# More right-half pairs by seven products, quarter sums in place with a third raw tile, and second attention heads spread over more ticks

## The chip, the cores and the metric

The kernel runs on one core of one Trainium2 chip. The metric is device time in microseconds (us) of one execution. A core has five engines with queues of their own: TensorE (PE; its weight loads are listed as PEld), VectorE (DVE), ScalarE (ACT), GpSimd (POOL) and SyncE (SP), the last of which here only issues loads and stores. They meet through semaphores. Sixteen DMA engines move data between HBM and the on-chip memory.

## The reference

Two decoder layers on `x` of 256 tokens by 2048 columns, in float32:

```python
for l in range(DEPTH):                       # 2
    h = rmsnorm(x, attn_norm_g[l])
    q, k, v, gate_b, gate_c, conv_in = split(h @ w_in[l])       # 6 x 1024 columns
    q, k = rmsnorm over 64-wide half heads
    attn = diff_attention(q, k, v, lam, rel_bias)               # 8 heads, softmax1 - lam * softmax2, causal
    attn = rmsnorm(attn, subln_g[l]) * (1 - lam_init)
    conv = gate_b * short_conv3(gate_c * conv_in, conv_w[l])
    x = x + concat([attn, conv]) @ w_out[l]
    hm = rmsnorm(x, mlp_norm_g[l]) @ w_up[l]                     # 8192 columns
    x = x + square(relu(hm)) @ w_down[l]
```

## The kernel before

**Precision.** TensorE multiplies in a reduced form of float32, so every operand is split into a high part and the rest (ScalarE writes the high part, VectorE subtracts). A product is three terms (`TERMS`): high x high, high x low, low x high. Weights come from HBM as raw tiles and are split on the way: `whi`/`wlo` (L302, L303), `uhi`/`ulo` for w_up (L816, L817), `b1h`, `b2h`, `t13h`, `t24h` and their `l` parts for w_down by seven (L839, L840).

**A layer.** `mixer` runs q, k, v for the first four heads, then for the second four (`linear`, L386), then gate_C and conv_in in turn (`linear_t`: gc, ci, L408), gate_B (gb) and the output projection (o). `mlp` then runs the up stage and the right half.

**Background work.** TensorE's order is the order of the program, written by hand. Work that lies beside the main matmuls is a set of generators in `Background`; each `work.tick()` in a linear loop (16 in each `linear` and `linear_t`, 4 in each call of `columns`) counts the generators' waits down, and one that is due emits its next piece, its matmuls too, at that place. `attention` (with `pace` 1 for the first half of the heads, 2 for the second) runs four heads through `staggered`: each does its scores (`sc`), waits 10 ticks, transposes the probabilities (`ptp`), waits 4 ticks, multiplies by v (`av`); the last one also normalises all four (`an`) and after another wait transposes them into `cat` (`atp`). `Norm.chunk` makes a quarter of the next norm's tiles (`nT`). The order of the other engines is fixed when the program is built, by a simulated timeline; where `late` (`keep` in `quarters`) is used, it stays as written. Weight jobs are made `AHEAD` = 3 before they are taken.

**w_down by seven products.** The hidden columns are worked as 32 pairs of 128 (256 rows of w_down). For one pair, tokens in two halves and hidden rows in two halves make a 2 x 2 matrix of activations, and hidden rows by two stretches of 512 output columns a 2 x 2 matrix of weights. Their product takes eight products of 128 x 128 x 512, or seven after sums of quarters (a scheme like Strassen's). Each product is three matmuls, so an ordinary pair is 24 matmuls and one by seven is 21. `square` makes the sums of the activations once (L974 to L977). `quarters` makes those of the weights: `plain` loads the raw tile (L826, 1 MB) and splits b11 and b21, b22; `sums` computes t1, t3 (L853), t2 (L856) and t4 (L857) into a tile `t` with one buffer; `more` splits t2 and t4.

The left half of the output (`col` 0) is done during the up stage: 30 pairs by seven, two pairs behind the up columns (`LAG`), and the last two in the ordinary way. The hidden values are written to HBM (`hid`, or `hid7` for pairs that will go by seven on the right). In the right half they are read back: first pairs 30 and 31, then pairs 0 to 2 x `BLK` - 1 one by one (L1074 ordinary, L992 by seven, which pairs `SEVEN` lists), then the rest as blocks of two pairs by `columns` (L1143; `by_token`, L1131, for the last). `seven_onto` adds the seven accumulators to x (L1055, L1047, L1063). Read-back tiles `fb` come from `apool` (four buffers, shared with the norm tiles `nT`), the first block's from `fpool`. Raw tiles of w_down by seven come from `dpool` (`draw`, two buffers), those of w_up and of ordinary pairs from `upool` (`uraw`, four).

The pools of `mixer` and `mlp` use the same memory in turn, so the first loads of one wait for the last readers of the other.

Of the kernel before, what the change touches and what calls it, by code (L numbers as in the profile page):

```python
# [9 lines left out]
F32 = mybir.dt.float32  # L10
F32R = mybir.dt.float32r
# [4 lines left out]
P = 128  # L16
# [12 lines left out]
CH = 512  # L29
# [6 lines left out]
NB2 = DFF // (KG * P)  # L36


SEVEN = (2, 4, 7, 9, 12, 14, 17, 19, 22)
BLK = 12  # L40

TERMS = ((0, 0), (0, 1), (1, 0))
REL = 2 * S - P - 1
# [45 lines left out]
def staggered(pieces, apart):  # L89

    entries = [[i * apart, p] for i, p in enumerate(pieces)]
    while entries:
        for e in list(entries):
            if e[0] <= 0:
                try:
                    e[0] = max(1, next(e[1]))
                except StopIteration:
                    entries.remove(e)
                    continue
            e[0] -= 1  # L100
        if entries:
            yield 1
# [3 lines left out]
def trunk(ctx: ExitStack, tc: tile.TileContext, x, w_in, w_out, conv_w, q_norm_g, k_norm_g,  # L106
          lambda_q1, lambda_k1, lambda_q2, lambda_k2, subln_g, attn_norm_g, mlp_norm_g,
          w_up, w_down, rel_bias, selector, out):
    nc = tc.nc
# [3 lines left out]
    apool = ctx.enter_context(tc.tile_pool(name="apool", bufs=4))  # L113
# [12 lines left out]
    def bank(name):  # L126
        return ps.tile([P, CH], F32, tag="bank", name=name)

    def wide(name):
        return nat.tile([P, CH], F32, tag="wide", name=name)  # L130

    work = Background()
# [451 lines left out]
    def attention(l, qT, kT, kL, v, h0, dst, bias, tmp, pace):  # L584
# [3 lines left out]
        parts = dst.open()  # L588
# [5 lines left out]
        def unit(i):  # L594
            h = h0 + i
# [30 lines left out]
            for t in range(NT):  # L626
# [2 lines left out]
                                               nlam[:, l:l + 1], op0=ALU.mult, op1=ALU.mult)  # L629
                nc.vector.scalar_tensor_tensor(p[:, w], s[:, 1, w], c[:, t:t + 1], s[:, 0, w],  # L630
                                               op0=ALU.mult, op1=ALU.add)
            yield 10
            tp = bank(f"ptp{h}")
            for b in range(3):
                nc.tensor.transpose(tp[:, b * P:(b + 1) * P], p[:, b * P:(b + 1) * P], ident)
            pT = tmp.tile([P, 2, 3 * P], F32R, tag="pT", name=f"pT{h}", bufs=1)
            nc.scalar.activation(pT[:, 0], tp[:, :3 * P], AF.Copy)
            nc.vector.tensor_sub(pT[:, 1], tp[:, :3 * P], pT[:, 0].bitcast(F32))
            yield 4

            av = ps.tile([P, CH], F32, tag="av", name=f"av{h}", bufs=1)
            av = av.rearrange("p (t n c) -> p t n c", t=NT, n=2)
# [19 lines left out]
            f = rstd_of(flat, P, f"a{h0}", 4 * NT)  # L662
# [3 lines left out]
            for t in range(NT):  # L666
# [3 lines left out]
                    ao[:, t].rearrange("p (g d) -> p g d", d=P),  # L670
                    f2[:, :, t:t + 1].to_broadcast([P, 4, P]), op=ALU.mult)
                an_.append(an)
            yield 12 if pace == 1 else 18
            for t in range(NT):
                tp = bank(f"atp{h0}_{t}")
                for b in range(4):
# [7 lines left out]
                    op0=ALU.mult, op1=ALU.subtract)  # L684
                yield 2

        yield from staggered([unit(i) for i in range(4)], 8)
        dst.ready = True

    def conv(l, q, u, cv, norm):  # L690
# [99 lines left out]
    def mlp(l, mnorm, last):  # L790

        norm = None if last else Norm(0, l + 1)
        mT = mnorm.tiles
        with ExitStack() as scope:
            upool = scope.enter_context(tc.tile_pool(name="upool", bufs=4))
            fpool = scope.enter_context(tc.tile_pool(name="fpool", bufs=2))
            dpool = scope.enter_context(tc.tile_pool(name="dpool", bufs=2))
            spool = scope.enter_context(tc.tile_pool(name="spool", bufs=1))
            work.start(mnorm.factors(), 1)

# [2 lines left out]
            raws, forms = {}, {}  # L803
# [27 lines left out]
            def quarters(i, col=0):  # L831


                keep = late if i == 0 or (i == SEVEN[0] and col) else lambda ins: None

                def parts(src, tag, bufs):
                    hi = spool.tile(list(src.shape), F32R, tag=f"{tag}h", name=f"{tag}h", bufs=bufs)
                    lo = spool.tile(list(src.shape), F32R, tag=f"{tag}l", name=f"{tag}l", bufs=bufs)
                    keep(nc.scalar.activation(hi, src, AF.Copy))  # L839
                    keep(nc.vector.tensor_sub(lo, src, hi.bitcast(F32)))  # L840
                    return hi, lo

                def plain():
                    raw = forms["raw"] = load_rows(i, col).rearrange("p k (n c) -> p k n c", n=2)
                    h1, l1 = parts(raw[:, 0, 0], "b1", 2)
                    h2, l2 = parts(raw[:, 1], "b2", 2)
                    return (h1, l1), (h2[:, 0], l2[:, 0]), (h2[:, 1], l2[:, 1])

                def sums():
                    raw = forms["raw"]  # L850
                    t = forms["t"] = spool.tile([P, 4, CH], F32, tag="t", name="t")

                    keep(nc.vector.tensor_sub(t[:, 0:2], raw[:, :, 1], raw[:, 0]))  # L853
                    h, lw = parts(t[:, 0:2], "t13", 1)

                    keep(nc.vector.tensor_add(t[:, 2], t[:, 1], raw[:, 0, 0]))  # L856
                    keep(nc.vector.tensor_sub(t[:, 3], raw[:, 1, 0], t[:, 2]))  # L857
                    return (h[:, 0], lw[:, 0]), (h[:, 1], lw[:, 1])

                def more():  # L860
                    h, lw = parts(forms["t"][:, 2:4], "t24", 1)
                    return (h[:, 0], lw[:, 0]), (h[:, 1], lw[:, 1])

                if (i, col) == (0, 0):
                    made = {}
                    forms["plain"] = lambda: made.update(p=plain())
                    forms["sums"] = lambda: made.update(s=sums())
                    return lambda: made["p"], lambda: made["s"], more
                return plain, sums, more
# [21 lines left out]
            for i in range(NP - LAG, NP):  # L891
# [5 lines left out]

            order = [(b - n, n) for b in range(BLK, NB2) for n in range(2)
                     if BLK <= b - n < NB2 - 1]

# [12 lines left out]
            def blocks_of(order):  # L913
                for b, n in order:
                    box = []
                    four(b, n, 0, box)
                    four(b, n, 2, box)

            blocks_of([(NB2 - 1, 0), (NB2 - 1, 1)])
            for i in range(2 * BLK):  # L920
                if i in SEVEN:
                    weights.jobs += quarters(i, 2 * CH)
                    continue
                box = []
                for k in range(2):
# [5 lines left out]
            hid = {i: dram.tile([P, 2, 4 * P], F32R, name=f"hid{l}p{i}")  # L931
                   for i in range(NP - LAG) if i not in SEVEN}
            hid7 = {i: dram.tile([P, 8 * P], F32, name=f"hid{l}s{i}") for i in SEVEN}

# [27 lines left out]
            def square(i, h):  # L962
# [9 lines left out]
                if i < NP - LAG:  # L972
# [4 lines left out]
                    nc.vector.tensor_sub(h[:, S4], h[:, A12], h[:, S2])  # L977
                if i in SEVEN:
                    nc.gpsimd.dma_start(hid7[i], h.rearrange("p a c -> p (a c)"))
# [16 lines left out]
            for i in range(NP):  # L996
                j = i - LAG
                end = i == NP - 1
                h = fpool.tile([P, 8, P], F32, tag="h", name="h", bufs=1)
# [12 lines left out]
                for c in range(2):  # L1012
# [15 lines left out]
                    if j >= 0 and c == 0:  # L1028
                        b11, b21, b22 = weights.take()
                        t1, t3 = weights.take()  # L1030
                        f = fs[j]
# [5 lines left out]
                    elif j >= 0:  # L1037
                        t2, t4 = weights.take()
                        f = fs[j]
# [10 lines left out]
            def seven_onto(n):  # L1050


                x11, x21, x12, x22 = (xs[n + i][:, t] for i in range(2) for t in range(NT))
                e1, e2, e3, e4 = wide("e1"), wide("e2"), wide("e3"), wide("e4")
                nc.scalar.activation(e1, prods[1], AF.Copy, scale=mnorm.scale)  # L1055
                onto(e2, prods[6], e1)
                onto(e4, prods[5], e2)
                onto(x22, prods[5], x22)
                onto(e3, prods[7], e2)

                def add():
                    for dst, v in ((x11, e1), (x12, e4), (x21, e3), (x22, e3)):
                        nc.vector.tensor_add(dst, dst, v)  # L1063

                return add
# [23 lines left out]
            def pair(i, f=None, at=0):  # L1089

                if f is None:
                    f = apool.tile([P, 2, 8, P], F32R, tag="a", name="fb")
                if i not in SEVEN:
                    nc.gpsimd.dma_start(
# [7 lines left out]

            def block(b):

                pool, tag = (fpool, "f") if b == BLK else (apool, "a")
                f = pool.tile([P, 2, 8, P], F32R, tag=tag, name="fb")
                for j in range(2):
                    pair(2 * b + j, f, 4 * j)
                return f
# [40 lines left out]
            for n in range(2):  # L1150
                columns(lambda k, pa, t: fs[NP - LAG + k // 2][:, pa, k % 2 * 2 + t], n, start=True)
            for i in range(2 * BLK):
                if i + 1 < 2 * BLK:
                    fs[i + 1] = pair(i + 1)
# [5 lines left out]
                start, end = i == SEVEN[0], i == SEVEN[-1]  # L1160
# [6 lines left out]
                t2, t4 = weights.take()  # L1167
# [4 lines left out]
                    if n == 5:  # L1172
                        work.tick()
                work.tick()
            seven_onto(2)()
            if not last:
                work.start(norm.chunk(0, 2), 6)
                work.start(norm.chunk(1, 2), 11)

            for b, n in order:  # L1180
                if n == 0 and b + 1 < NB2 - 1:
                    blocks[b + 1] = block(b + 1)
                units = lambda k, pa, t, f=blocks[b]: f[:, pa, 2 * k + t]
                if last and (b, n) == order[-1]:
                    by_token(units, n)
                else:
                    columns(units, n, stop=(b == NB2 - 2))
                if b == NB2 - 2:
                    for t in range(NT):
                        onto(xs[2 + n][:, t], accs[n][:, t], xs[2 + n][:, t])  # L1190
                    if last:
                        store(2 + n)
                    else:
                        work.start(norm.chunk(2 + n, 2))
        return norm

    norm = Norm(0, 0)
# [10 lines left out]
    for l in range(DEPTH):  # L1208
        mnorm = mixer(l, norm, first_loads if l == 0 else lambda weights: None)
        norm = mlp(l, mnorm, l == DEPTH - 1)  # L1210
# [31 lines left out]
```

## Time and profile before

| | us |
|---|---|
| median of 3 runs | 2151.07 |
| lowest, highest | 2148.47, 2151.32 |
| profiled execution | 2151.32 |
| its span, first to last instruction | 2149.5 |

| stage, from the trace's windows | window, us | PE busy, us | DVE busy, us | ACT busy, us | GB/s |
|---|---|---|---|---|---|
| layer 1, second heads, gc, ci | 1200 to 1260 | 58.89 | 46.26 | 40.70 | 159 |
| layer 1, gc, ci | 1260 to 1320 | 57.47 | 38.83 | 29.15 | 243 |
| layer 1, start of the up stage | 1500 to 1560 | 57.70 | 54.04 | 40.42 | 240 |
| layer 1, right half | 2020 to 2080 | 60.00 | 53.12 | 36.34 | 302 |

The granted TensorE clock is 1.00 in all of them. In the profile a group's row reads: line, engine, operation, output <- inputs, shapes, count | busy us, mean ns | idle time before it and what ended most of it. A timeline's row reads: start, length, engine, line, operation, output <- inputs, shape, count [idle before it <- what ended it]. A wait's row reads: engine and what waited <- what it waited for: total us, times, longest. Matmuls are pipelined, so one row's length (about 0.39 us for 512 columns) is more than its share of TensorE's time.

### The profile page before, as it was taken

Reading aid. Unit: us, or ns where it says so; the run is one execution under the profiler, and the core shown is the slowest. Engines: PE = TensorE matmul, PEld = TensorE weight load, DVE = VectorE, ACT = ScalarE, POOL = GpSimd, SP = SyncE. Lnnn points to the kernel's source line nnn. Section 1 sums busy time; section 2 is a strip of 40 time slices with the busy share of each in tenths; the row PEclk is TensorE's granted clock in tenths of the full one; section 3 lists DMA queues with packets and bytes.
Section 4 is the critical chain, followed back from the end, with each engine's and each line's share of the span. In section 5 each row is a group of like instructions: output and inputs, shape, how many; then the busy total and the mean of one; then the engine's idle time right before and its main releaser. Section 6 shows DMA issues by size and latency. Waiting matters only on the chain. (4 is left out here: it accounts for less than half of the span.)

```text
span 2149.5 us, 28983 instructions
## 1 busy us (share of the span) xinstructions
PE 2134.0 (99%) x10934; PEld 1819.9 (85%) x10934; DVE 1678.6 (78%) x2297; ACT 1308.2 (61%) x1767; POOL 169.8 (8%) x226
## 2 busy tenths in 40 slices
PE   9999999999999999999999999999999999999999
PEld 8888888888888888888888888888888888888887
DVE  6777655799889888798566776557888888888984
ACT  6666445666666666565566654446666666665652
POOL 3111100000000000011110111000000000001110
PEclk9999999999999999999999999999999999999999
DMA  8555766577777777798665566656777777777984
GB/s 271 179 160 171 246 186 187 190 244 230 233 232 231 229 227 234 241 318 288 210 178 176 166 197 215 187 176 204 241 233 223 240 229 226 235 225 262 335 264 137
DMA packets 298524, 475.98 MB, mean 221 GB/s; under 512 B 10803, under 2 KB 191621, under 8 KB 298384
## 3 DMA queue, kind: packets, MB, share of 16 engines
q1 hardware_dynamic: 268768, 406.88, 60.4%
q0 software_dynamic: 29568, 67.24, 9.4%
q8 instruction: 85, 1.39, 0.3%
q14 instruction: 55, 0.45, 0.1%
q10 hardware_dynamic: 48, 0.02, 0.0%
HBM read 440.52 MB, written 33.58 MB: 221 GB/s over the span
## 5 line engine op out<-in xcount | busy, mean ns | idle before, releaser
L303 DVE TENSOR_TENSOR wlo<-raw,whi 128x1024 fp32r<-128x1024 f32 x286 | 352.2, 1234 | 252.3 <-ACT whi L302 245.8
L302 ACT ACTIVATE whi<-raw 128x1024 fp32r<-128x1024 f32 x286 | 303.1, 1060 | 341.1 <-PE o L386 73.6
L949 PE MATMUL upc<-nT,uhi 128*128 128x512 f32 x1920 | 477.7, 391 | 0.6 <-ACT ev L959 0.6
L816 ACT ACTIVATE uhi<-uraw 128x1024 fp32r<-128x1024 f32 x256 | 271.2, 1060 | 280.3 <-PE upc L949 260.4
L949 PEld LDWEIGHTS upc<-nT,uhi 128*128 128x128 f32 x1920 | 352.7, 188 | 69.2 <-ACT ev L959 1.1
L817 DVE TENSOR_TENSOR ulo<-uraw,uhi 128x1024 fp32r<-128x1024 f32 x256 | 312.9, 1223 | 109.3 <-ACT uhi L816 105.3
L949 PEld LDWEIGHTS upc<-nT,ulo 128*128 128x128 f32 x1920 | 261.9, 190 | 18.7
L949 PE MATMUL upc<-nT,ulo 128*128 128x256 f32 x1920 | 267.7, 282 | 0.0
L386 PE MATMUL o<-whi,cat 128*128 128x512 f32 x512 | 159.5, 390 | 0.0
L1074 PE MATMUL dn<-whi,fb 128*128 128x512 f32 x480 | 151.1, 389 | 0.0
L386 PEld LDWEIGHTS o<-whi,cat 128*128 128x128 f32 x512 | 96.1, 188 | 19.7
L302 ACT ACTIVATE whi<-uraw 128x1024 fp32r<-128x1024 f32 x60 | 63.7, 1061 | 75.7 <-PE dn L1074 70.7
L1074 PEld LDWEIGHTS dn<-whi,fb 128*128 128x128 f32 x480 | 90.1, 188 | 18.7
L386 PE MATMUL o<-wlo,cat 128*128 128x512 f32 x256 | 99.6, 389 | 0.0
L840 DVE TENSOR_TENSOR t13l<-t,t13h 128x1024 fp32r<-128x1024 f32 x78 | 95.5, 1224 | 4.0 <-ACT t13h L839 2.2
L839 ACT ACTIVATE b2h<-draw 128x1024 fp32r<-128x1024 f32 x78 | 82.5, 1058 | 24.9 <-PE pr L992 22.2
L840 DVE TENSOR_TENSOR b2l<-draw,b2h 128x1024 fp32r<-128x1024 f32 x78 | 95.5, 1224 | 2.1 <-ACT b2h L839 2.1
L840 DVE TENSOR_TENSOR t24l<-t,t24h 128x1024 fp32r<-128x1024 f32 x78 | 95.2, 1221 | 1.4 <-ACT t24h L839 0.3
L853 DVE TENSOR_TENSOR t<-draw 128x1024 f32<-128x1024 f32 x78 | 95.3, 1221 | 0.4
L992 PE MATMUL pr<-t13h,f 128*128 128x512 f32 x240 | 93.8, 391 | 0.0
L1074 PE MATMUL dn<-wlo,fb 128*128 128x512 f32 x240 | 93.4, 389 | 0.0
L303 DVE TENSOR_TENSOR wlo<-uraw,whi 128x1024 fp32r<-128x1024 f32 x60 | 73.2, 1224 | 21.1 <-ACT whi L302 20.9
(408 smaller groups left out, 4138.6 us busy)
## 6 DMA issues: line engine op xcount, KB each, us to landing
uraw<-in_w_up_dram SPq DMA_DIRECT2D x128, 1024.0 KB, 6.5
raw<-in_w_in_dram SPq DMA_DIRECT2D x191, 512.0 KB, 4.0
draw<-in_w_down_dram SPq DMA_DIRECT2D x82, 1024.0 KB, 5.3
raw<-in_w_out_dram SPq DMA_DIRECT2D x64, 512.0 KB, 3.6
uraw<-in_w_down_dram SPq DMA_DIRECT2D x30, 1024.0 KB, 6.3
raw<-in_w_down_dram SPq DMA_DIRECT2D x16, 1024.0 KB, 5.2
hid0p<-f POOLq DMA_DIRECT2D x21, 512.0 KB, 6.4
fb<-hid0p POOLq DMA_DIRECT2D x21, 512.0 KB, 5.9
```

Of the source, the lines that this page charges most:

```text
L302: pair = (nc.scalar.activation(hi, raw, AF.Copy), nc.vector.tensor_sub(lo, raw, hi.bitcast(F32)))
L303: nc.vector.tensor_sub(lo, raw, hi.bitcast(F32)))
L386: nc.tensor.matmul(acc[:, t], a.ap[:, pa, k % KG, t * P:(t + 1) * P], (hi, lo)[pw][:, j], start=(k == 0 and n == 0), stop=(k == nk - 1 and ...
L816: pair = (nc.scalar.activation(hi, src, AF.Copy), nc.vector.tensor_sub(lo, src, hi.bitcast(F32)))
L817: nc.vector.tensor_sub(lo, src, hi.bitcast(F32)))
L839: keep(nc.scalar.activation(hi, src, AF.Copy))
L840: keep(nc.vector.tensor_sub(lo, src, hi.bitcast(F32)))
L853: keep(nc.vector.tensor_sub(t[:, 0:2], raw[:, :, 1], raw[:, 0]))
L949: nc.tensor.matmul(acc[:, 0] if part else acc, wt[:, k], a.ap[:, 0, k % KG] if part else a.ap[:, :, k % KG], start=(part == 0 and kh == 0 ...
L992: nc.tensor.matmul(prods[n], f[:, pa, a], b[pw], start=(start and m == 0), stop=(stop and m == 2))
L1074: nc.tensor.matmul(prods[p], f[:, pa, 2 * k + t], b[pw][:, n], start=(p in starts and k == 0 and m == 0), stop=(stop and k == 1 and m == 2))
```

## The change

It has six edits. (1) `SEVEN` is per layer: 10 right-half pairs by seven in layer 0 and 11 in layer 1 instead of 9 in both, and `BLK` is 13 and 14 instead of 12, so that 26 and 28 pairs are worked one by one. (2) `quarters` computes its sums in place, in the raw tile's own quarters: t1, t3 over b12, b22 by one operation with the outer dimension reversed, t2 over b11, t4 over b21. The tile `t` goes, and `dpool` has three buffers; both take 8 KB per partition, so the sum of the pools is the same. (3) The second four heads' waits are all multiplied by `pace`: 20, 8 and 24 ticks instead of 10, 4 and 18, and heads start 16 ticks apart instead of 8. (4) The first block's tile comes from `apool` like the others. (5) `seven_onto` is called right after the last pair by seven; in layer 0 one ordinary pair follows it, in layer 1 none. (6) The next layer's norm pieces start at other ticks.

```diff
-SEVEN = (2, 4, 7, 9, 12, 14, 17, 19, 22)
-BLK = 12
+SEVEN_AT = (2, 4, 7, 9, 12, 14, 17, 19, 22, 24, 27)
+BLK_AT = (13, 14)
...
-            yield 10
+            yield 10 * pace
             tp = bank(f"ptp{h}")
...
-            yield 4
+            yield 4 * pace
...
-            yield 12 if pace == 1 else 18
+            yield 12 * pace
...
-        yield from staggered([unit(i) for i in range(4)], 8)
+        yield from staggered([unit(i) for i in range(4)], 8 * pace)
...
     def mlp(l, mnorm, last):
+        BLK = BLK_AT[l]
+        SEVEN = [i for i in SEVEN_AT if i < 2 * BLK]
...
-            dpool = scope.enter_context(tc.tile_pool(name="dpool", bufs=2))
+            dpool = scope.enter_context(tc.tile_pool(name="dpool", bufs=3))
...
                 def sums():
                     raw = forms["raw"]
-                    t = forms["t"] = spool.tile([P, 4, CH], F32, tag="t", name="t")
-
-                    keep(nc.vector.tensor_sub(t[:, 0:2], raw[:, :, 1], raw[:, 0]))
-                    h, lw = parts(t[:, 0:2], "t13", 1)
-
-                    keep(nc.vector.tensor_add(t[:, 2], t[:, 1], raw[:, 0, 0]))
-                    keep(nc.vector.tensor_sub(t[:, 3], raw[:, 1, 0], t[:, 2]))
+                    t31 = raw[:, ::-1, 1]
+                    keep(nc.vector.tensor_sub(t31, t31, raw[:, 0, ::-1]))
+                    h, lw = parts(raw[:, :, 1], "t13", 1)
+
+                    t2, t4 = raw[:, 0, 0], raw[:, 1, 0]
+                    keep(nc.vector.tensor_add(t2, raw[:, 1, 1], t2))
+                    keep(nc.vector.tensor_sub(t4, t4, t2))
                     return (h[:, 0], lw[:, 0]), (h[:, 1], lw[:, 1])
 
                 def more():
-                    h, lw = parts(forms["t"][:, 2:4], "t24", 1)
+                    h, lw = parts(forms["raw"][:, :, 0], "t24", 1)
...
             def block(b):
-                pool, tag = (fpool, "f") if b == BLK else (apool, "a")
-                f = pool.tile([P, 2, 8, P], F32R, tag=tag, name="fb")
+                f = apool.tile([P, 2, 8, P], F32R, tag="a", name="fb")
...
                 work.tick()
-            seven_onto(2)()
+                if end:
+                    seven_onto(2)()
             if not last:
-                work.start(norm.chunk(0, 2), 6)
-                work.start(norm.chunk(1, 2), 11)
+                work.start(norm.chunk(0, 2), 4)
+                work.start(norm.chunk(1, 2), 8)
...
                     else:
-                        work.start(norm.chunk(2 + n, 2))
+                        work.start(norm.chunk(2 + n, (5, 2)[n]))
```

## The prediction, made before the changed kernel was run

> **What bounds the kernel now.** I read the page first, then the chain of waits, then the list of waits of TensorE's weight loads, and last the timelines around each of those waits. The page:
>
> ```profile
> span 2149.5 us, 28983 instructions
> PE 2134.0 (99%) x10934; PEld 1819.9 (85%) x10934; DVE 1678.6 (78%) x2297; ACT 1308.2 (61%) x1767; POOL 169.8 (8%) x226
> ```
>
> TensorE is busy nearly everywhere. The chain of waits (start, length, what) gives the price of a matmul and of a tick:
>
> ```profile
> 1304.63 11.17 PE gc L408 x64
> ...
> 2065.42 10.88 PE dn L1074 x48
> ```
>
> 48 matmuls of 512 columns take 10.88 us, so one costs 10.88/48 = 0.2267 us; this is what a removed matmul is worth. The 64 matmuls of one `linear_t` take 11.17 us and hold 16 ticks of the background work: one tick is 0.70 us there. What TensorE loses to waiting stands in the weight loads' waits (total us, times, longest):
>
> ```profile
> PEld pr L992 <- DVE f L982: 4.0, 2, 2.1
> PEld ptp L635 <- DVE s L630: 3.0, 6, 1.0
> PEld ci L408 <- ACT whi L302: 2.4, 2, 1.8
> PEld av L648 <- DVE pT L638: 1.8, 4, 0.7
> PEld sc L604 <- DVE cat L682: 1.7, 2, 0.9
> PEld upc L949 <- ACT ev L959: 1.1, 1, 1.1
> ```
>
> These are 14.0 us in both layers together. The change can win hardly more than these and its removed matmuls.
>
> **Seven products for more pairs.** An ordinary pair is 2 x 4 x 3 = 24 matmuls, a pair by seven is 7 x 3 = 21. Layer 0 gets one more such pair (24) and layer 1 two (24, 27). The other pairs below the new `BLK` only move from blocks, 48 matmuls for two pairs, to 24 each, which is the same. Removed: 3 x 3 = 9 matmuls, 9 x 0.2267 = **2.0 us**. The Trainium skill (TensorE: Matmul & The Clock Gate, section Back-to-back issue gap) gives about 131 ns for the sustained spacing at 512 columns; by that the same nine would bring an estimated 1.2 us. The chain shows 226.7 ns, and the measurement decides.
>
> The extra sevens load VectorE. The right half of layer 1, as a window (length; then busy us of PE, PEld, DVE, ACT, POOL; clock, DMA share, GB/s), and VectorE's groups in it:
>
> ```profile
> 1985.00:2105.00 120.00, 120.00 (x531) 99.36 (x530) 103.30 (x101) 70.98 (x74) 16.50 (x25) 1.00 0.89 301
> ```
> ```profile
> L303 DVE TENSOR_TENSOR wlo<-uraw,whi 128x1024 fp32r<-128x1024 f32 x30 | 36.6, 1224 | 10.2 <-ACT whi L302 10.1
> ...
> L1100 DVE TENSOR_TENSOR fb<-back,fb 128x1024 fp32r<-128x1024 f32 x8 | 9.8, 1220 | 0.2 <-ACT fb L1099 0.2
> L857 DVE TENSOR_TENSOR t<-draw,t 128x512 f32<-128x512 f32 x9 | 6.2, 690 | 0.2
> ```
>
> An ordinary pair asks VectorE for two `wlo`, 2.4 us. One by seven asks for five operations of 1024 elements (`b2l`, the first sum, `t13l`, `t24l`, `fb`) and three of 512: 5 x 1.22 + 3 x 0.69 = 8.2 us. The new list keeps two sevens in five pairs, so five pairs need 2 x 8.2 + 3 x 2.4 = 23.6 us of VectorE in (2 x 21 + 3 x 24) x 0.2267 = 25.8 us of TensorE: 91%, beside the window's 103.3/120 = 86% with TensorE full. The stretch gets longer, not denser, and an extra seven moves the same bytes (1 MB of weights, 512 KB of hidden values), so DMA stays at the window's 301 GB/s. Priced at nothing. If VectorE had no slack, each added seven would show 8.2 - 2.4 - 4.8 = 1.0 us, 3 us in all.
>
> **Second heads spread.** All `ptp` and `av` waits lie in the second half's heads, where TensorE comes back too early. TensorE's timeline, for the last head of layer 0:
>
> ```profile
> 187.40 0.40 PE L604 MATMUL sc<-kL,qT 128*128 128x128 f32 x2
> ...
> 197.09 0.83 PE L635 MATMUL ptp<-ident,s 128*128 128x128 f32 x3 [0.85 <-DVE s L630]
> ```
>
> From the end of the scores (about 187.6) to the transposes it took 9.5 us, for ten ticks, 7.0 us, and the other heads' matmuls between. Twenty ticks give 14 us, and eight ticks for `av` 5.6 instead of 2.8. The heads then start 16 ticks apart: the last at tick 9 + 48, and its `cat` is written by tick 113, within the 128 ticks of gc and ci and long before the output projection. No instruction is added. Bounds: nothing to 3.0 + 1.8 = 4.8 us; I take **4.3**, because a weight load's wait partly runs under the matmul before it. `sc` stays, since its tick is not moved. The `ci` wait has another origin. SyncE's queue, and ScalarE:
>
> ```profile
> 1273.99 7.39 SPq L809 DMA_DIRECT2D uraw<-in_w_up_dram  x4
> 1281.48 18.54 SPq L343 DMA_DIRECT2D raw<-in_w_in_dram  x8
> ```
> ```profile
> 1292.08 1.06 ACT L302 ACTIVATE whi<-raw 128x1024 fp32r<-128x1024 f32 x1 [7.80 <-DMA raw<-in_w_in_dram]
> ```
>
> Four early loads of 1 MB cut into the stream of input weights about when the second heads are done with the memory they get. The last head's normalised output moves from tick 47 to tick 85, 38 ticks or 27 us later, still inside gc and ci, so the same hole comes later: 0, with bounds of -2.4 (gone) and +2.4 (twice).
>
> **Third raw tile, sums in place.** At the start of each up stage ScalarE, in its fixed order, waits for a raw tile, and TensorE pays two steps later. Layer 1, by VectorE, SyncE's queue, ScalarE and TensorE:
>
> ```profile
> 1508.60 1.22 DVE L840 TENSOR_TENSOR t24l<-t,t24h 128x1024 fp32r<-128x1024 f32 x1
> ...
> 1514.61 1.22 DVE L840 TENSOR_TENSOR b2l<-draw,b2h 128x1024 fp32r<-128x1024 f32 x1
> ...
> 1516.88 0.69 DVE L857 TENSOR_TENSOR t<-draw,t 128x512 f32<-128x512 f32 x1
> ...
> 1523.82 1.22 DVE L853 TENSOR_TENSOR t<-draw 128x1024 f32<-128x1024 f32 x1
> ```
> ```profile
> 1507.24 10.11 SPq L809 DMA_DIRECT2D uraw<-in_w_up_dram  x2
> 1517.59 0.40 SPq L826 DMA_DIRECT2D draw<-in_w_down_dram  x1
> ```
> ```profile
> 1528.79 0.63 ACT L839 ACTIVATE b1h<-draw 128x512 fp32r<-128x512 f32 x1 [5.29 <-DMA draw<-in_w_down_dram]
> ```
> ```profile
> 1533.32 2.11 PE L949 MATMUL upc<-nT,uhi 128*128 128x512 f32 x8 [0.65 <-ACT ev L959]
> ...
> 1541.29 0.50 PE L992 MATMUL pr<-b1h,f 128*128 128x512 f32 x1 [1.66 <-DVE f L982]
> ```
>
> The load at 1517.59 is pair 4's (counted from 0). With two tiles it waits for pair 2's last sum, which ends at 1517.57. In place, a tile is held until its `t24l`, but with three the load needs only pair 1's, which ended at 1509.8. It can go 7.8 us sooner, more than the 5.29 us of waiting. The list shows `pr` waiting once in each layer. Both waits of this origin, 4.0 + 1.1 = 5.1 us, are the upper bound, 0 the lower; I take **4.3** for the reason given at the heads. Operation counts and shapes stay: one sum of 1024 and two of 512 elements per pair. A negative step on the outer dimension isn't in these rows; I price it as the plain operation, which it is nearest to, with a bound of twice the 1.22 us. In the up stage, where VectorE is fullest:
>
> ```profile
> 1560.00:1800.00 240.00, 240.00 (x1281) 207.46 (x1280) 212.72 (x288) 160.45 (x196) 9.35 (x15) 1.00 0.75 232
> ```
>
> 240 - 212.7 = 27.3 us are idle in 15 pairs, 1.8 us each, so that bound would still be covered there. The in-place sum adds one order: it has to follow `b2h` and `b2l` of its own pair. Pair 3's `b2l` ended at 1515.8 and its first sum began at 1523.8: that order is kept today. What falls away is the wait for the single `t`.
>
> **Around the end of the right half.** The final sums of the sevens (one ScalarE copy, four L1047, four L1063) move up; the next layer's norm pieces start at 4 and 8 ticks instead of 6 and 11, the third waits 5 instead of 2. The last of those sums, and the chain beside it:
>
> ```profile
> 2109.02 1.89 DVE L1063 TENSOR_TENSOR x<-x,e 128x512 f32<-128x512 f32 x3
> ```
> ```profile
> 2106.90 5.44 PE dn L1074 x24
> 2112.34 27.20 PE dn L1143 x120
> ```
>
> Today they end at 2110.9, 4.0 us after the last seven's products (2106.9). In layer 1 only 2 x 5.44 = 10.9 us of columns will follow them instead of 38. Three of the four `wlo` for these are made beforehand (`AHEAD`); the fourth comes behind the sums, at about +5.4 us, and is needed at 5.44 + 6 x 0.2267 = +6.8. Hidden, with 1.4 us to spare; without that cover 1 to 2 us. In layer 0 an ordinary pair and 21.8 us of columns cover the sums and the norm pieces. The first block's two loads move on POOL's queue behind a slot that pairs give free every 5 us; behind them waits only the next block's load, not due for 10 us. All at nothing.
>
> **Sum.** 2.0 + 4.3 + 4.3 = 10.6 us. The profiled execution took 2151.32 us (span 2149.5 and 1.8 around it), 0.25 us above the median of 2151.07. Forecast: 2151.3 - 10.6 = 2140.7, say **2141 us**.
>
> **Rivals.** (1) The load does not move up: SyncE issues in order, and pair 4's load stands right behind a w_up load that left only about 1517 (the two issues that last 10.11 us). If that order stays, the up stage's waits stay: 2151.3 - 6.3 = 2145. Against it: one such load stands between two w_up loads, the next ahead of both or behind, as each comes free. 0.12. (2) The spread only moves its waits, because ScalarE, stopped for 7.8 us by the hole, delays the last heads: 2145 too. 0.1; both together, 2149, 0.08. (3) On the other side: the in-place sum falls behind `t13h`, which waits for TensorE, in VectorE's fixed order, and so comes late in every pair of the up stage. 60 pairs at 0.65 us, the smaller wait above, are 39 us: 2141 + 39 = 2180. It makes the kernel slower from (10.6 + 4.3)/60 = 0.25 us a pair on. For it: VectorE is 89% busy there. Against: 1.8 us idle per pair, and 8 us between `b2l` and the sum. 0.1. (4) The sums behind pair 27 come late: 2 us more, inside the range.
>
> **How the numbers follow.** Forecast 0.6, (1) 0.12, (2) 0.1, both 0.08, (3) 0.1. A measurement of this kernel tells about 0.2%, 4.3 us, from no change, so faster means below 2146.8. Faster: the forecast and most of (1) and (2), 0.76. Same: 2149 and its neighbours, 0.13. Slower: 0.11. Low end: all waits but `sc` gone, 2151.3 - 2.0 - 4.8 - 5.1 - 2.4 = 2137, less one; high end 2150, which takes in (1), (2) and both and leaves out (3).
>
> **What would show it.** Right: no `ptp`, `av`, `pr` and `upc` rows in the weight loads' waits, nine matmuls of 512 columns fewer, pair 4's load ahead of the w_up load and ScalarE's 5.29 us gone. Wrong: a `pr` or `upc` wait in every pair of the up stage, or VectorE near 100% there; a wait of dn L1131 at the end of layer 1; a longer `ci` wait.

## The result and the profile after

| | before | after |
|---|---|---|
| median of 5 runs each, us | 2151.17 | 2171.31 |
| ratio after/before, 95% interval | | 1.0096, 1.0081 to 1.0110 |
| profiled execution's span, us | 2149.5 | 2169.5 |

The changed kernel is 20 us slower; 2141 was forecast. The page of the kernel after, with the same lines as before:

```profile
span 2169.5 us, 28871 instructions
PE 2139.9 (99%) x10925; PEld 1822.0 (84%) x10925; DVE 1715.7 (79%) x2315; ACT 1331.0 (61%) x1776; POOL 163.3 (8%) x226
```

The nine matmuls are gone (x10934 before, x10925 after). The waits of the weight loads after (total us, times, longest):

```profile
PEld pr0r L996 <- ACT t24h L841: 4.8, 1, 4.8
PEld pr1r L996 <- ACT t24h L841: 4.6, 1, 4.6
PEld pr L996 <- issue: 2.7, 2, 1.4
PEld pr0r L996 <- DVE t13l L842: 2.7, 1, 2.7
PEld pr1r L996 <- DVE t13l L842: 2.7, 1, 2.7
PEld pr1r L996 <- DVE t24l L842: 2.6, 1, 2.6
PEld pr0r L996 <- DVE t24l L842: 2.6, 1, 2.6
PEld pr L996 <- DVE f L986: 2.3, 2, 1.1
PEld pr L996 <- DVE t13l L842: 1.8, 2, 1.1
PEld sc L604 <- DVE cat L682: 1.7, 2, 0.9
PEld upc L953 <- ACT ev L963: 1.6, 3, 1.0
...
PEld pr L996 <- ACT t13h L841: 0.8, 1, 0.8
...
PEld ci L408 <- ACT whi L302: 0.2, 1, 0.2
```

Three things are seen here. `ptp` and `av` (4.8 us before) have no row, and `ci` went from 2.4 to 0.2. The rows of the up stage (`pr` and `upc`) hold 9.2 us where they held 5.1. And six rows are new: `pr0r` and `pr1r`, the accumulators of the right half, one set for each layer, wait once each for `t13l`, `t24h` and `t24l`: 20.0 us in all. Windows around the two places (start and end; length; busy us and count of PE, PEld, DVE, ACT, POOL; granted clock, DMA share, GB/s):

```profile
928.00:950.00 22.00, 13.45 (x43) 9.72 (x42) 16.37 (x19) 7.02 (x8) 1.95 (x3) 0.69 0.62 198
...
2006.00:2030.00 24.00, 15.70 (x51) 11.42 (x51) 18.04 (x19) 7.92 (x9) 1.96 (x3) 0.72 0.60 197
```

At full clock 22 and 24 us hold 99 and 108 matmuls (a mended kernel below shows these counts); here are 43 and 51. The missing 113 are worth 113 x 0.2267 = 25.6 us: 20.0 of waiting, by the weight loads' rows, and the other 5.6 put down to the lower clock. The books of the change by rows: -2.0 (nine matmuls), -4.8 (`ptp`, `av`), -2.2 (`ci`), +4.1 (start of the up stage), +25.6 (these two places) = +20.7, against +20.0 between the spans. Not in these books is a clock of 0.84 between 415 and 425 us, at the start of layer 0's up stage.

What happens at 930 us is seen by putting the two timelines side by side (start, length, engine, line, operation). It is the first pair by seven of the right half, pair 2. Before, VectorE and then ScalarE:

```profile
910.38 1.22 DVE L853 TENSOR_TENSOR t<-draw 128x1024 f32<-128x1024 f32 x1
```
```profile
911.64 1.06 ACT L839 ACTIVATE t13h<-t 128x1024 fp32r<-128x1024 f32 x1
...
918.04 1.06 ACT L839 ACTIVATE t24h<-t 128x1024 fp32r<-128x1024 f32 x1 [0.69 <-DVE t L857]
...
923.27 1.05 ACT L839 ACTIVATE b2h<-draw 128x1024 fp32r<-128x1024 f32 x1
```

The first sum ran at 910.38, **ahead** of the pair's own `b1h` and `b2h` (`b2h` at 923.27, `b1h` right before it): with a tile of its own it needed only the raw tile. The kernel after, VectorE, ScalarE and TensorE:

```profile
925.83 1.22 DVE L856 TENSOR_TENSOR draw<-draw 128x1024 f32<-128x1024 f32 x1
...
936.72 1.29 DVE L861 TENSOR_TENSOR draw<-draw 128x512 f32<-128x512 f32 x2
...
940.19 1.22 DVE L842 TENSOR_TENSOR t24l<-draw,t24h 128x1024 fp32r<-128x1024 f32 x1
```
```profile
921.60 1.05 ACT L841 ACTIVATE b2h<-draw 128x1024 fp32r<-128x1024 f32 x1
...
934.42 1.06 ACT L841 ACTIVATE t13h<-draw 128x1024 fp32r<-128x1024 f32 x1 [2.99 <-PE pr0r L996]
937.43 1.06 ACT L841 ACTIVATE t24h<-draw 128x1024 fp32r<-128x1024 f32 x1 [1.95 <-DVE draw L861]
```
```profile
932.78 0.50 PE L996 MATMUL pr0r<-t13l,fb 128*128 128x512 f32 x1 [2.27 <-DVE t13l L842]
...
938.54 0.80 PE L996 MATMUL pr0r<-t24h,fb 128*128 128x512 f32 x1 [4.16 <-ACT t24h L841]
941.47 0.80 PE L996 MATMUL pr0r<-t24l,fb 128*128 128x512 f32 x1 [2.12 <-DVE t24l L842]
942.06 0.63 PE L996 MATMUL pr0r<-t24h,fb 128*128 128x512 f32 x1
942.48 0.63 PE L996 MATMUL dn<-t24h,fb 128*128 128x512 f32 x1
...
947.80 0.40 PE L1078 MATMUL dn<-wlo,fb 128*128 128x512 f32 x1
948.03 0.62 PE L1078 MATMUL dn<-whi,fb 128*128 128x512 f32 x2
```

In place, a sum overwrites quarters that `b2h` and `b2l` read, so it has to follow them. `keep` (L836, for the right half's first pair by seven) holds those splits at their late place. It is written on the sums too, before and after, but before, the sums still ran ahead of the splits; in place they can't: 925.8 instead of 910.4. The `t13h` at 934.42 is already pair 4's; it waits 2.99 us for TensorE to leave the single `t13` buffer and stands ahead of pair 2's `t24h`, which TensorE needs first. Even then `t24h` waits another 1.95 us for pair 2's last sum (L861, at 936.72), which stands on VectorE behind the first sums and splits of later pairs; VectorE is busy for 20.79 of the 21 us from 921 to 942.

### The profile page after: what moved, and what is told of

It reads as the page before. It is cut to its first block, busy times and chain, and to the rows that moved or that the text cites. A ratio compares the mean times of both kernels' runs of the same rounds, so it can differ in the third digit from the quotient of the medians.

```text
span 2169.5 us, 28871 instructions
## 1 busy us (share of the span) xinstructions
PE 2139.9 (99%) x10925; PEld 1822.0 (84%) x10925; DVE 1715.7 (79%) x2315; ACT 1331.0 (61%) x1776; POOL 163.3 (8%) x226
## 4 chain that ended last, share of the span: by engine, by line
PE 96%; DVE 2%; ACT 1%; issue 1%; DVEq 0%; ACTq 0%
PE upc L953 30%; PE pr L996 13%; PE o L386 8%; PE dn L1078 8%; PE ci L408 4%; PE gb L408 4%; PE k L386 4%; PE q L386 4%; PE v L386 4%; PE gc L408 4%; PE dn L1146 2%; PE dn L996 2%; PE pr1r L996 1%; PE pr0r L996 1%; PE upw L953 1%; PE up L953 1%
## 5 line engine op out<-in xcount | busy, mean ns | idle before, releaser
L303 DVE TENSOR_TENSOR wlo<-raw,whi 128x1024 fp32r<-128x1024 f32 x274 | 342.5, 1251 | 220.9 <-ACT whi L302 219.4
L302 ACT ACTIVATE whi<-raw 128x1024 fp32r<-128x1024 f32 x274 | 290.4, 1060 | 307.4 <-PE o L386 73.6
L1078 PE MATMUL dn<-whi,fb 128*128 128x512 f32 x528 | 168.6, 394 | 0.0
L1078 PEld LDWEIGHTS dn<-whi,fb 128*128 128x128 f32 x528 | 101.0, 191 | 21.5
L841 ACT ACTIVATE t24h<-draw 128x1024 fp32r<-128x1024 f32 x81 | 86.1, 1063 | 37.2 <-PE pr L996 16.4
L842 DVE TENSOR_TENSOR t24l<-draw,t24h 128x1024 fp32r<-128x1024 f32 x81 | 99.0, 1222 | 9.1 <-ACT t24h L841 6.5
L1078 PE MATMUL dn<-wlo,fb 128*128 128x512 f32 x264 | 104.2, 395 | 0.0
L842 DVE TENSOR_TENSOR t13l<-draw,t13h 128x1024 fp32r<-128x1024 f32 x81 | 99.0, 1222 | 6.5 <-ACT t13h L841 3.3
L856 DVE TENSOR_TENSOR draw<-draw 128x1024 f32<-128x1024 f32 x81 | 99.0, 1223 | 1.7
L841 ACT ACTIVATE t13h<-draw 128x1024 fp32r<-128x1024 f32 x81 | 86.0, 1062 | 17.7 <-PE pr0r L996 6.2
```

Source lines behind the costliest of these rows:

```text
L302: pair = (nc.scalar.activation(hi, raw, AF.Copy), nc.vector.tensor_sub(lo, raw, hi.bitcast(F32)))
L303: nc.vector.tensor_sub(lo, raw, hi.bitcast(F32)))
L856: keep(nc.vector.tensor_sub(t31, t31, raw[:, 0, ::-1]))
L1078: nc.tensor.matmul(prods[p], f[:, pa, 2 * k + t], b[pw][:, n], start=(p in starts and k == 0 and m == 0), stop=(stop and k == 1 and m == 2))
```

## The experiments

Theory S: the in-place sums fall behind the held splits at the two places where `keep` fixes the order, the right half's first pair by seven and pair 0 of the up stage. Its rivals: the in-place operations are slow in themselves; the extra pairs or the spread heads cost; the earlier loads of the third tile collide with something. Beside each time stands the median of the kernel before, run on the same chip.

**The sums back in a tile of their own.** The changed kernel with the second edit undone:

```diff
-dpool = ... bufs=3
+dpool = ... bufs=2
-                    nc.vector.tensor_sub(t31, t31, raw[:, 0, ::-1])
+                    t = spool.tile([P, 4, CH], F32, tag="t", name="t")
+                    nc.vector.tensor_sub(t[:, 0:2], raw[:, :, 1], raw[:, 0])
...
```

> The changed kernel with the second edit alone undone: the sums go back into a tile of their own, two raw tiles. Theory S (in the right half's first pair by seven the in-place sums have to follow b2h and b2l, which are held at their place in the program, so t13h, t13l, t24h and t24l come too late): the waits of pr0r and pr1r (about 20 us in the changed kernel, with some 5 us of lower clock behind them) are gone, and what is left are the gains of the heads (-3.9 to -4.8), of ci (-2.3) and of nine matmuls (-2.0): 2141 to 2144 us, a ratio to the kernel before of 0.995 to 0.997. Rival L (the longer stretch or the denser list of sevens overloads VectorE or DMA): the waits stay, 2165 to 2173.

Measured: 2141.18 us, before 2154.17, ratio 0.9944 (0.9927 to 0.9961). The weight loads' waits:

```profile
PEld pr L994 <- DVE f L984: 4.0, 2, 2.0
PEld sc L604 <- DVE cat L682: 1.7, 2, 0.9
```

Below these two stand only rows of 1.1 us and less. The rows of `pr0r` and `pr1r` have gone, and so have `ptp`, `av` and `ci`. The second edit alone turns a gain of 12 us into a loss of 20 (each against the kernel before on its own chip).

**That edit alone on the kernel before.** The opposite of the run above:

```diff
-dpool = ... bufs=2
+dpool = ... bufs=3
+                    t31 = raw[:, ::-1, 1]
+                    nc.vector.tensor_sub(t31, t31, raw[:, 0, ::-1])
...
```

> The kernel before with the second edit alone: sums in place and three raw tiles, all else as it was. Theory S: both waits of about 10 us at the first pair by seven of the right half, some 5 us of lower clock and about 3 us at the start of the up stages: 2176 to 2181 us, ratio 1.012 to 1.014. Rival L: 2146 to 2153, as the lists of sevens are those of before.

Measured: 2182.26 us, before 2154.17, ratio 1.0134 (1.0119 to 1.0149). The waits at both places come back with nearly the same numbers, with nine sevens and the old heads; the longest of the weight loads' rows:

```profile
PEld pr1r L994 <- ACT t24h L839: 4.8, 1, 4.8
```

The operations themselves are no slower. The groups by form, of the kernel after and of the kernel before (busy us, mean ns):

```profile
L856 DVE TENSOR_TENSOR draw<-draw 128x1024 f32<-128x1024 f32 x81 | 99.0, 1223 | 1.7
```
```profile
L853 DVE TENSOR_TENSOR t<-draw 128x1024 f32<-128x1024 f32 x78 | 95.3, 1221 | 0.4
```

**The hold taken away on the right**, in the changed kernel and, as a control, in the kernel before:

```diff
-keep = late if i == 0 or (i == SEVEN[0] and col) else lambda ins: None
+keep = late if i == 0 else lambda ins: None
```

> The changed kernel with one condition taken out: the splits and sums of the first pair by seven on the right are no longer held at their place in the program. Theory S: they go ahead by some 20 us of TensorE's time, the waits of pr0r and pr1r vanish with the lower clock behind them, and the time is 2171 - 20 - 5 = 2146 us (2143 to 2149), ratio 0.996 to 0.999. Rival L, and a rival R (the operations in the raw tile are slower, or the tile held longer delays loads): the waits stay or move to the next seven, 2160 to 2173.

> The kernel before with the same condition taken out, as a control: there the sums do not depend on the splits and no wait stands at that place, so theory S gives no change, 2149 to 2153 us, ratio 0.999 to 1.001. If the condition itself costs time whatever the sums do, it is faster by several us.

Measured: 2164.26 us, ratio 1.0051 (1.0036 to 1.0066), and for the control 2161.47, ratio 1.0038 (1.0023 to 1.0053); before 2154.17. Both miss. In the changed kernel the waits of `pr0r` and `pr1r` are gone, but others take their place:

```profile
PEld pr L1078 <- DVE f L986: 9.1, 2, 5.0
PEld pr L1078 <- ACT f L985: 5.3, 2, 2.9
```

Freed, pair 2's splits and sums are put before 900 us, ahead of the last activations `f` of the left half, pair 31. VectorE's timeline of this kernel there:

```profile
898.73 1.22 DVE L842 TENSOR_TENSOR t24l<-draw,t24h 128x1024 fp32r<-128x1024 f32 x1
...
907.98 0.69 DVE L986 TENSOR_TENSOR f<-h,f 128x512 fp32r<-128x512 f32 x1
```

In the changed kernel the same `f` ran at 899.86. The control shows that the hold was worth something before the change too, some 8 us (5 to 11); it cannot just be dropped. This doesn't speak against S, but it doesn't show it either: the place between the two had to be tried.

**The first seven between the two places.** The changed kernel, with pair 2's whole set of tiles emitted in one piece behind `f` of pair 31 and ahead of the columns of pairs 30 and 31, still held in order:

```diff
+                if i == SEVEN[0] and col:
+                    first = {}
+                    forms["first"] = lambda: first.update(p=plain(), s=sums(), m=more())
+                    return lambda: first["p"], lambda: first["s"], lambda: first["m"]
...
+            forms["first"]()
             fs = {30: fs[30], 31: fs[31], 0: pair(0)}
```

> The changed kernel, in which the splits, sums and second splits of the right half's first pair by seven (pair 2) are emitted as one piece ahead of the columns of pairs 30 and 31, about 21 us of TensorE earlier, and still in the order of the program. Theory S (the in-place sums stand behind held splits, and pair 4's t13h stands ahead of pair 2's t24h): the waits of pr0r and pr1r for t24h, t13l and t24l (4.8 + 4.6 + 2.7 + 2.7 + 2.6 + 2.6 us) go, the f of pair 31 does not become late as in the run that freed the condition, the granted clock stays at 1.00 around the place, and the time is 2144 to 2150 (the changed kernel less 20 and less about 5 of clock). Rival (the loads that the third tile lets in, not the order, make the first pair late): the waits stay or move, and the time stays above 2158.

Measured: 2148.92 us, before 2152.59, ratio 0.9985 (0.9975 to 0.9994), as S has it. The windows of the two places:

```profile
928.00:950.00 22.00, 22.00 (x99) 18.23 (x98) 20.76 (x21) 12.87 (x14) 3.20 (x5) 1.00 1.01 353
2006.00:2030.00 24.00, 24.00 (x108) 19.88 (x107) 20.55 (x21) 14.49 (x15) 3.22 (x5) 1.00 0.98 338
```

TensorE is full, at full clock, with the third raw tile still there: so it is not the loads that this tile lets in that made the first pair late. What was moved costs little at its new place (`dn` for `wlo`, waits of 2.5 us in the two layers together). The waits of `pr` at the start of the up stage stay as in the kernel after.

**The other held place, the same way.** In addition `sums` of the up stage's pair 0 emitted ahead of the `square` of its activations:

```diff
+                    forms["sums"]()
                     fs[0] = square(0, h)
-                    forms["sums"]()
```

> As the run before, and at the start of the up stage the sums of pair 0 are emitted ahead of the square of pair 0's activations. Theory S also for the up stage's start: the waits at pair 0 (2.6 us in layer 0, 4.6 in layer 1) go, so 3 to 7 us less than the run before, 2138 to 2145. Rival (those waits are for the raw load and the norm, not for the order): the same as the run before within 1 us. If the third raw tile is worth the 4.3 us of the prediction, this run is under the kernel with the separate tile of sums (0.9944 of before); if not, it is level with it.

Measured: 2157.17 us, before 2152.59, ratio 1.0019 (1.0010 to 1.0028): 8 us worse than the run before, a miss. The weight loads' first row, and the operation that was late:

```profile
PEld pr L1000 <- issue: 10.8, 2, 5.6
```
```profile
424.08 1.23 DVE L990 TENSOR_TENSOR f<-h,f 128x1024 fp32r<-128x1024 f32 x1 [1.18 <-ACT f L989]
```

The first product needs `f` as well, which ran at 420.23 in the run before. Sums put ahead of activations only change which of the two is late; the operation's own wait, 1.18 us, is the only idle time of VectorE between 404 and 426 us in this run.

**Pair 1 behind pair 0.** Without the tile `t`, pair 1's sums no longer wait for pair 0's, and VectorE's timeline of the first-seven-earlier kernel shows one of them far ahead of pair 0's activations (in the kernel before, the first two sums of layer 0's up stage ran at 419.54 and 429.78, both behind them):

```profile
407.68 1.22 DVE L856 TENSOR_TENSOR draw<-draw 128x1024 f32<-128x1024 f32 x1
...
420.23 1.22 DVE L990 TENSOR_TENSOR f<-h,f 128x1024 fp32r<-128x1024 f32 x1
```

So pair 1's pieces were held too, its sums behind its own activations; and the same with two raw tiles, and the version with sums aside, on one chip:

```diff
+                        if i == 1:
+                            hand[1]["sums"]()
...
-dpool = ... bufs=3
+dpool = ... bufs=2
```

> The changed kernel with pair 2 of the right half made ahead of the columns of pairs 30 and 31, and with pair 1 of the up stage held in program order: its in-place sums behind the square of pair 1's activations instead of ahead of pair 0's. Theory S2: the waits at pair 0 (about 3 us in layer 0, 4 in layer 1 in the run with only the first change) come from pair 1's sums (L856, L860, L861, 2.6 us of VectorE) that overtook pair 0's activations once no tile of sums held them back; they go, 2140 to 2144. Rival: they come from something else, and the time stays at 2147 to 2150; or pair 1's own sums are then late and a wait of pr for t13h takes their place, 2146 to 2156.

> The run before with two raw tiles instead of three, the sums still in place. It measures what the third raw tile is worth where the order is mended. Prediction's term: the load of a pair waits again for the last reader of the pair two before, and waits like those of the kernel before at pair 3 of the up stage (pr for f, 1.7 us a layer, with 0.8 beside it) return, so 3 to 6 us slower than the run before. Rival (the in-place sums set the raw tile free as late as ever, or the third tile is hidden): within 1 us of it.

> The changed kernel with the separate tile of sums and two raw tiles, as in the first experiment, here beside the two runs before it on the same chip: ratio 0.993 to 0.996 of before. If the mended in-place sums with a third tile are worth what the prediction said of them, the first run of this call is 3 to 5 us below this one; if the third tile only pays back what the longer way of the sums costs, the two are within 2 us.

| kernel | median, us | ratio to before (2153.21) |
|---|---|---|
| sums in place, mended, three raw tiles | 2147.46 | 0.9973, 0.9961 to 0.9984 |
| the same, two raw tiles | 2222.29 | 1.0320, 1.0306 to 1.0334 |
| sums in a tile of their own, two raw tiles | 2141.00 | 0.9942, 0.9928 to 0.9955 |

The first is the rival's outcome: the waits at pair 0 went (its `f` ran at 414.81 instead of 420.23), which shows that pair 1's pieces, made too early, had caused them, and pair 1's own came instead.

```profile
PEld pr L1001 <- DVE t13l L843: 3.8, 2, 1.9
```

The second, forecast at 3 to 6 us, cost 75. Its weight loads' first row, the largest of ScalarE's waits, then ScalarE's timeline in the middle of the up stage:

```profile
PEld upc L958 <- ACT ev L968: 79.4, 50, 2.4
```
```profile
ACT b1h L842 <- DMA draw<-in_w_down_dram: 153.8, 59, 3.8
```
```profile
650.20 0.63 ACT L842 ACTIVATE b1h<-draw 128x512 fp32r<-128x512 f32 x1 [3.64 <-DMA draw<-in_w_down_dram]
...
653.58 0.58 ACT L968 ACTIVATE ev<-upc 128x512 f32<-128x512 f32 x1
```

In most pairs (47 of these 59 waits lie in the two up stages, which have 60 pairs by seven) `b1h` waits for its load, the eviction `ev` of the next column stands behind it, and TensorE waits for that one's bank. By the code, a raw tile is held in place until `t24l` instead of until the last sum; with that, two tiles no longer suffice. The third tile is what sums in place **cost**; the time that it may win lies behind that.

**The two good parts alone.** The spread of the second heads alone on the kernel before, and the version with sums aside without that spread:

```diff
-            yield 10
+            yield 10 * pace
...
```

> The kernel before with the second heads' waits spread, and nothing else. Theory P (the prediction's term): ptp 3.0 and av 1.8 go, sc stays; the ci wait of 2.4 was priced 0 and went in the changed kernel, so -4.3 to -6.7 us, ratio 0.997 to 0.998. Rival (the waits move to other pieces of the stage): between -1 and +1 us.

> The changed kernel with the separate tile of sums, two raw tiles and the old pace of the second heads: what is left are the further pairs by seven, the longer stretch of pairs, the fifth right tile and the moved norm pieces. Theory P: nine matmuls of 0.2267 us fewer, -2.0 us, and ptp and av waits as before; ratio about 0.999. With the clocked gap that the Trainium skill states for back-to-back matmuls it would be -1.2 us. Rival R (the first block and the norm pieces start otherwise, so the ends of the layers gain or lose): below -4 or above 0 us.

Measured, before 2152.59: 2144.45 us, ratio 0.9958 (0.9946 to 0.9971), and 2148.32, ratio 0.9977 (0.9968 to 0.9986). In microseconds the spread brings 9 (6 to 12), more than the 4.3 to 6.7 expected, and the rest of the change 5 (3 to 7), more than the 2.0 expected; the version with both brings 12. The spread's own profiled execution has a span of 2144.5, 5.0 below that of before, and shows where: of its weight loads' rows none is left of `ptp` and `av`, `sc` stays at 1.7, and `ci` has 1.3 instead of 2.4.

```profile
PEld ci L408 <- ACT whi L302: 1.3, 2, 0.8
```

The `ci` row is no proof of the spread: without it, this row has 1.1 us in the second of these kernels and 3.0 in the kernel before with the sums in place.

A third raw tile beside the separate tile of sums doesn't fit into the memory of a partition, so what it would bring there stays open.

## Why the prediction was wrong

**The step that failed** is the one on the in-place sums: "that order is kept today". It was read off pair 3 of the up stage and taken for every pair. It didn't hold for the right half's first pair by seven, whose first sum ran 13 us ahead of its `b2h`. The sentence after it, "What falls away is the wait for the single `t`", was put at nothing too; in fact this wait had kept pair 1's sums behind pair 0's at the start of the up stage. Undoing this edit alone, and doing it alone, shows the whole loss.

- **Sums in place with a third raw tile, priced -4.3, measured +25.6 and +4.1.** What was forecast of the load was right: pair 4's went out at 1516.08, 18.2 us after the up stage's first product in layer 1 (1497.9), where before it was 27.3 us (1517.59 after 1490.3): 9.1 us sooner, 7.8 were forecast. ScalarE's list of waits, in the kernel before and in the kernel after, shows what it was to bring (total us, times, longest):

```profile
ACT b1h L839 <- DMA draw<-in_w_down_dram: 19.3, 7, 5.3
```
```profile
ACT b1h L841 <- DMA draw<-in_w_down_dram: 1.0, 2, 0.5
```

  The waits of `pr` at pair 3 did go, but the gain was overpaid where the pipelines start: 12.8 us at each of the two places on the right, 4 at the starts of the up stages. With the order mended on the right and at pair 0 the edit still costs 6.5 us against the separate tile (2147.46 to 2141.00); the rows of `pr`, `upc` and `dn` differ by 7.0 (11.7 to 4.7). The reversed outer step was priced rightly, at nothing.
- **Rival (3)** came nearest: sums that come late, a `t13h` that waits for TensorE, and the right sign. But what held the sums were the splits, and it was `t24h` that stood behind the waiting `t13h`; place and price were wrong as well: not 60 times 0.65 us but twice 12.8. In this kernel the added order cost nothing in the middle of the up stage (from 1570 to 1800 us of the kernel after TensorE is busy for 230.00 of 230 us) and showed only where a pipeline starts.
- **Rivals (1) and (2)**, that the load stays where it was and that the spread only moves its waits, did not come about: the load moved, and no row of `ptp` or `av` is left.
- **Seven products, -2.0.** Nine matmuls fewer, as forecast, and VectorE stayed below its limit (59.82 us busy from 2030 to 2100, 58.33 before; after the first pair by seven no row of the right half waits for it). With the other small edits the run gave 5 us (3 to 7). Between the profiled executions it is 3.4, which the nine matmuls (2.0) and a `ci` row shorter by 1.3 nearly fill; why `ci` shrank was not told apart.
- **Second heads, -4.3.** The mechanism was right, and `sc` stayed at 1.7 as said. `ci`, priced at nothing, lost 1.1 us with the spread alone and 2.2 in the full change, near its bound of -2.4, but 1.3 also without the spread, so its cause stays open. By the traces the spread brings 5.0; the timed runs say 9 (6 to 12).
- **End of the right half, 0.** No wait of a `dn` stands in the list after, so this was right.
- **The lower clock** was in no step: a fifth of the loss at the two places.

That the version without the second edit takes the predicted 2141 is chance in part: the 4.3 us of the raw tile are not in it, the larger yield of the other two is.

## What to carry to other kernels

Computing in place trades a buffer for an order: it makes each write wait for every reader of the old content and keeps the source alive until the last reader of the new one. List both for every instance of the loop, and check the first instances and those whose order is pinned, not a steady one. A scratch tile that looks spare may be what holds later work back, as the single `t` did for pair 1.

## What the chip showed that was not expected

The waits of 10 us cost TensorE more than 10. Of the rows that close its timeline above, the two at 942.06 and 942.48 start 0.42 us apart, where 0.2267 is usual; the two at 947.80 and 948.03 start 0.23 apart again. The granted clock is 1.00 from 930.4 to 933.8 us and 0.50 from 933.9 to 947.5. The windows put the loss beside the waits at 56 x 0.2267 - 10.1 = 2.6 and 57 x 0.2267 - 9.9 = 3.0 us. The Trainium skill (TensorE: Matmul & The Clock Gate, section What's actually happening) says that the clock falls to half after an idle window of about 3.4 us and is back after as long a stretch of work. The trace agrees with the half speed but not with the lengths: the clock was at half before the wait of 4.16 us began (at 934.4), behind a wait of only 2.27, and the way back took some 6 us from the last wait.

Still shorter waits lowered it in one layer and not in the other. The kernel with only the first seven earlier has the same two waits of TensorE at pair 0 of both layers, 1.19 and 0.70 us, in layer 1 with two more of 0.33 and 0.81 behind them, and these windows around them:

```profile
415.00:425.00 10.00, 8.11 (x35) 6.14 (x33) 7.84 (x12) 5.75 (x8) 0.75 (x1) 0.83 0.83 265
...
1485.00:1495.00 10.00, 6.96 (x33) 4.98 (x32) 9.00 (x14) 6.37 (x9) 0.76 (x1) 1.00 0.78 251
```

The clock fell in layer 0 and stayed full in layer 1, where the waits were longer in sum. Why is not shown.
